# Half of the weight sums and left factors of the seven-product gemms made in earlier stages and kept in DRAM; 32 seven-product quads instead of 26

## The chip, the core and the metric

The kernel runs on one core of a Trainium2 chip. Its time is the device time of one execution in microseconds (us). Five engines run their own in-order instruction queues: TensorE (PE, matmuls; PEld is its weight load), VectorE (DVE), ScalarE (ACT), GpSimd (POOL) and SyncE (SP), which here issues nearly all DMA transfers. Semaphores tie the queues together.

## What is computed

One layer of a hybrid block for 256 tokens of width 2048: a norm, one wide projection `w_in`, an attention branch with three dilated windows, a state-space (SSM) branch with a chunked scan, a gated merge of both, and an output projection. Cut to what matters here:

```python
hn = rms_norm(x, norm_w)
proj = hn @ w_in                      # q, k, v, z_a, z_s, xbc, dt, g_a, g_s
o_a = attention(q, k, v) * silu(z_a)
y = rms_norm((scan(conv(xbc), dt) + d_skip * xs) * silu(z_s), ssm_norm_w)
merged = sigmoid(g_a) * (o_a @ w_attn_branch) + sigmoid(g_s) * (y @ w_ssm_branch)
x = x + merged @ w_out
return rms_norm(x, final_norm_w)
```

Everything is float32. The largest part of the work is the product of the 256 tokens with 2048 or 4096 rows of weights, for all the outputs.

## The kernel before

**Split products.** Each float32 operand is split into a high part (`h`, ScalarE, a copy rounded to the PE's fp32r type) and a low part (`l`, VectorE, the rest), and a product is three matmuls: high by high, high by low, low by high (`triple` in `gemm_pair`; in `gemm_a` the first two are one matmul of 512 columns, the third one of 256).

**Weights.** The host lays all weights out as 481 units of 128 x 1024 floats (512 KB) in the order of their use (`weight_plan`, `lay_weights`). `load` (L207) fetches a unit into one of four places (tag `w`) by a DMA on SP's queue; `unit` (L213) splits it into one of four places each for `h` and `l` (lines 222 and 223). The splits are put up to 120 instructions ahead of their place in the program (`L_AHEAD`). A place of `w` comes free when its `l` is made, places of `h` and `l` when their matmuls are done.

**Stages,** in the order of the PE: the first projections; the gates `gs`; the SSM part (`project` of `B`, `C`, and of 31 tiles each of `xs` and `zs`, in eight groups; beside it convolutions, decays and the scan of each group run on ScalarE and VectorE, set off by a count of ticks, `after`); then the pair stages `ssm` (columns 0 and 1024 on, `y` times `w_ssm_branch`), `v`, and half of `ga`; the attention part (`q`, `k`, `za` of 16 heads); the rest of `ga`; `attn`; `out`. The order of each engine's instructions is fixed when the program is made: a list scheduler goes by the order of the code, moved by priorities, and by its own estimate of times.

**Pair gemms and quads.** In the pair stages `gemm_pair` (L363) works in steps `q` of two row blocks of 128 (two units, 1 MB), for 2 halves of the tokens and 2 blocks of 512 columns. A plain step makes the 2x2x2 block products as 8 triples, 24 matmuls of 512 columns. A step listed in `S_QUADS` is a quad: a Winograd form with 7 triples, 21 matmuls. It needs sums of the weight blocks B11, B12, B21, B22 (line 432: B12-B11 and B12-B22 as one instruction of 1024 columns; 437: B22 minus the first; 438: B21 minus that) and four left factors, sums of the token blocks (`turn_x`, lines 355 to 360), each split into high and low again. In a quad the weight sums take places `t13` (one), `ht` and `lt` (two each) in the pool `mul`. There are 26 quads: 5 and 6 in the two halves of `ssm`, 2 and 3 in `v`, 3 in `ga`, 3 in `attn`, 2 and 2 in `out`. The left factors of `ssm` and `v` are made once per `q`, at the head of the stage that first uses them.

**Places in SBUF.** `yo0` holds the first half of `y` (`yT0`) and later `oaT`, the attention's output; `yo1` holds the raw input and norm work (`early`), later the second half of `y` (`yT1`, from group 4 on), later `v` and the `ga` gate (`vth`).

Of the kernel before, what the change touches and what calls it, by code (L numbers as in the profile page):

```python
# [31 lines left out]
MUL_PAD = 112  # L32
# [11 lines left out]
}  # L44

# [61 lines left out]
def lay_weights(mats):  # L107
    out = np.empty((N_UNITS, P, UNIT), np.float32)
    for tag, form, src, off, n_kt, w in PLAN:
# [6 lines left out]
        if form == "p":  # L116
# [3 lines left out]
            for q in range(n // 2):  # L120
                f = FIRST[tag] + 2 * q
                if q in S_QUADS[tag]:
                    out[f] = np.concatenate([m[q, 0, :, 0], m[q, 1, :, 1]], axis=1)
                    out[f + 1] = np.concatenate([m[q, 0, :, 1], m[q, 1, :, 0]], axis=1)
                else:
                    out[f : f + 2] = m[q].reshape(2, P, UNIT)
# [46 lines left out]
def hybrid_block(ctx: ExitStack, tc: tile.TileContext, wall, xt, x, pk_d, cst_d, fw_d, out):  # L173
# [15 lines left out]
    lead.tile([P, 8], F32, name="fill", tag="fill")  # L189
# [15 lines left out]
    on_unit = {}  # L205

# [6 lines left out]
    def unit(n, shape):  # L213
# [10 lines left out]
        if n in on_unit:  # L224
            on_unit.pop(n)(h[:, 0:1].bitcast(F32))
# [3 lines left out]
    def split(src, hi, lo, scale=1.0):  # L229
# [3 lines left out]
        else:  # L233
            ve.scalar_tensor_tensor(lo, src, scale, hi.bitcast(F32), ALU.mult, ALU.subtract)

# [35 lines left out]
    def gemm_dt(src):  # L271
# [8 lines left out]
        for u, tag in enumerate("hl"):  # L280
# [4 lines left out]
            if n in on_unit:  # L285
                on_unit.pop(n)(hl[:, 0, 0, 0:1].bitcast(F32))
            ve.tensor_tensor(hl[:, :, 1], w[:, ks], hl[:, :, 0].bitcast(F32), ALU.subtract)
            for kk in range(half_kt):
                kt = u * half_kt + kk
                pe.matmul(  # L290
                    acc, hl[:, kk].rearrange("p n m -> p (n m)"), src[:, kt, :], start=(kt == 0), stop=(kt == KT - 1)
# [6 lines left out]
    def gemm_first(tag, prepare, load_on):  # L298
        name = f"{tag[0]}{tag[1]}"
        accs = [bank("g", 4, f"ps_{name}_{j}") for j in range(4)]  # L300
        for u in range(KT // UB):
# [6 lines left out]
            for kk in range(UB):  # L308
                kt = u * UB + kk
                m = yT[0][:, kt, :]  # L310
# [37 lines left out]
    def turn_x(pool, bufs, temp, x, spare=0):  # L348


        sx = pool.tile([P, 2, 4 - spare, P], F32R, name=f"sx{now[0]}", tag="sx", bufs=bufs)
# [9 lines left out]
        parts = [(sx[:, 0, n], sx[:, 1, n]) for n in range(4 - spare)]  # L361
        if spare:
            own = x[:, 0, P:S], x[:, 0, S + P :]  # L363
            split(s[:, 0], *own)
            parts.insert(0, own)
        split(s[:, spare:], sx[:, 0], sx[:, 1])
        return parts

    def gemm_pair(tag, x_of, n_kt, sxs, swap, extra={}, close=1):
# [20 lines left out]
        for q in range(n_q):  # L390
            tick()
            if q in extra:
                extra[q]()
# [20 lines left out]
            for m in (n, n + 1):  # L414
                if m not in loaded:
                    load(m)
            wa, wb = loaded.pop(n), loaded.pop(n + 1)
# [11 lines left out]
            with tc.high_priority(L_AHEAD):  # L429
                t13 = mul.tile([P, UNIT], F32, name=f"t13_{n}", tag="t13", bufs=1)  # L430
                b12 = wb[:, :512].unsqueeze(1).to_broadcast([P, 2, 512])
                ve.tensor_tensor(two(t13), b12, two(wa), ALU.subtract)
# [600 lines left out]
```

## Time and profile before

| what | value |
|---|---|
| median of 3 runs | 1394.38 us (1394.28 to 1395.56) |
| span of the profiled execution | 1392.9 us (1.5 us under the median) |
| ScalarE busy | 811.5 us (58%) |
| GpSimd busy | 32.1 us (2%) |
| DMA moved | 272.33 MB, mean 196 GB/s |
| HBM read, written | 268.86 MB, 2.16 MB |

The span runs from the first to the last instruction of one execution; the runs' times hold 1.5 us around it. Busy shares are means over stages with different limits. A window's row gives, for a stretch of the span, the busy time of PE, PEld, DVE, ACT and POOL with their instruction counts, then the clock granted to the PE (1.00 is full), the DMA engines' busy share and GB/s. A row of a group gives line, engine, operation, what is written and read, shapes and count, then busy us and mean ns of one, then idle time of the engine before it and what ended it. A row of waits gives who waited for whom, us in total, times and the longest.

### The profile page before, as it was taken

The page shows a single profiled execution, that of the slowest core. Times are in us where ns is not written, and L with a number is a line of the kernel's source. Part 1 is how long each engine was busy: PE and PEld are TensorE (multiplying, and loading weights), DVE is VectorE, ACT ScalarE, POOL GpSimd, SP SyncE. Part 2 cuts the span into 40 slices and gives each one's busy share as a digit, 9 for nine tenths or more (in the row PEclk, how much of TensorE's full clock was granted, in tenths as well). Part 3 has the DMA queues.
Part 4 walks back from the last instruction along what each step waited for, and adds up shares of the span by engine and source line. Part 5 has one row for each costly group of instructions (what it writes and reads, how often), then busy time and mean ns, then how long its engine had stood idle before and what let it go on. Part 6 is the DMA issues. An engine that isn't in the chain of part 4 may idle for free.

```text
span 1392.9 us, 19889 instructions
## 1 busy us (share of the span) xinstructions
PE 1381.8 (99%) x7308; PEld 1176.8 (84%) x7308; DVE 1086.8 (78%) x1622; ACT 811.5 (58%) x1258; POOL 32.1 (2%) x86
## 2 busy tenths in 40 slices
PE   9999999999999999999999999999999999999997
PEld 7888888888888888888888888888888888888885
DVE  6897887776787787798988988766676666487887
ACT  7656676675667586665554555554554544454454
POOL 1300000000000000000000000000000000000010
PEclk9999999999999999999999999999999999999999
DMA  8766675756566665656666566655555655667564
GB/s 328 243 196 185 197 215 163 221 185 204 172 212 174 208 189 180 194 181 211 192 206 202 187 212 191 217 174 174 168 174 174 181 170 176 199 212 250 172 198 136
DMA packets 78210, 272.33 MB, mean 196 GB/s; under 512 B 8800, under 2 KB 9376, under 8 KB 77728
## 3 DMA queue, kind: packets, MB, share of 16 engines
q1 hardware_dynamic: 77392, 269.88, 61.9%
q8 instruction: 57, 0.93, 0.3%
q10 hardware_dynamic: 720, 1.18, 0.2%
q14 instruction: 41, 0.34, 0.1%
HBM read 268.86 MB, written 2.16 MB: 195 GB/s over the span
## 4 chain that ended last, share of the span: by engine, by line
PE 98%; DVE 1%; DMA 0%; issue 0%; ACT 0%; SPq 0%; POOL 0%; POOLq 0%; DVEq 0%
PE ps_zs L265 8%; PE ps_xs L265 8%; PE ps_zs L268 4%; PE ps_za L265 4%; PE ps_k L265 4%; PE ps_q L265 4%; PE ps_xs L268 4%; PE ps_ssm L384 3%; PE ps_ssm L385 3%; PE ps_ssm L386 3%; PE ps_q L268 2%; PE ps_k L268 2%; PE ps_za L268 2%; PE ps_gs L345 2%; PE ps_gs L343 2%; PE ps_gs L344 2%
## 5 line engine op out<-in xcount | busy, mean ns | idle before, releaser
L223 DVE TENSOR_TENSOR l<-w,h 128x1024 fp32r<-128x1024 f32 (+1 forms) x432 | 522.8, 1213 | 231.0 <-ACT h L222 229.3
L222 ACT ACTIVATE h<-w 128x1024 fp32r<-128x1024 f32 (+1 forms) x432 | 452.8, 1051 | 407.6 <-issue 104.5
L265 PE MATMUL ps_zs<-XT,h 128*128 128x512 f32 x496 | 174.6, 394 | 0.0
L265 PE MATMUL ps_xs<-XT,h 128*128 128x512 f32 x496 | 174.0, 393 | 0.0
L268 PE MATMUL ps_zs<-XT,l 128*128 128x256 f32 x496 | 139.2, 281 | 0.0
L268 PE MATMUL ps_xs<-XT,l 128*128 128x256 f32 x496 | 138.9, 280 | 0.0
L265 PEld LDWEIGHTS ps_zs<-XT,h 128*128 128x128 f32 x496 | 93.0, 187 | 21.3
L265 PEld LDWEIGHTS ps_xs<-XT,h 128*128 128x128 f32 x496 | 92.9, 187 | 20.9
L268 PEld LDWEIGHTS ps_zs<-XT,l 128*128 128x128 f32 x496 | 93.5, 188 | 1.2 <-issue 1.2
L268 PEld LDWEIGHTS ps_xs<-XT,l 128*128 128x128 f32 x496 | 93.5, 189 | 0.0
L265 PE MATMUL ps_q<-XT,h 128*128 128x512 f32 x256 | 92.3, 404 | 0.0
L265 PE MATMUL ps_k<-XT,h 128*128 128x512 f32 x256 | 89.8, 395 | 0.0
L265 PE MATMUL ps_za<-XT,h 128*128 128x512 f32 x256 | 89.7, 394 | 0.0
L268 PE MATMUL ps_q<-XT,l 128*128 128x256 f32 x256 | 71.1, 278 | 0.0
L268 PE MATMUL ps_za<-XT,l 128*128 128x256 f32 x256 | 71.0, 278 | 0.0
L268 PE MATMUL ps_k<-XT,l 128*128 128x256 f32 x256 | 71.0, 277 | 0.0
L385 PE MATMUL ps_ssm<-l,yT 128*128 128x512 f32 x168 | 65.3, 390 | 0.0
L386 PE MATMUL ps_ssm<-h,yT 128*128 128x512 f32 x168 | 65.0, 389 | 0.0
L384 PE MATMUL ps_ssm<-h,yT 128*128 128x512 f32 x168 | 57.5, 390 | 0.0
L265 PEld LDWEIGHTS ps_za<-XT,h 128*128 128x128 f32 x256 | 48.0, 188 | 11.3
L265 PEld LDWEIGHTS ps_k<-XT,h 128*128 128x128 f32 x256 | 48.0, 188 | 11.2
L265 PEld LDWEIGHTS ps_q<-XT,h 128*128 128x128 f32 x256 | 48.1, 188 | 10.9
(520 smaller groups left out, 2984.3 us busy)
## 6 DMA issues: line engine op xcount, KB each, us to landing
w<-in_wall SPq DMA_DIRECT2D x480, 512.0 KB, 3.8
acb<-acum_d SPq DMA_DIRECT2D x32, 256.0 KB, 3.6
th_s<-in_x SPq DMA_DIRECT2D x4, 512.0 KB, 6.5
vth<-in_x SPq DMA_DIRECT2D x1, 2048.0 KB, 9.3
early<-in_xt SPq DMA_DIRECT2D x7, 256.0 KB, 6.9
fw<-in_fw SPq DMA_DIRECT2D x1, 1024.0 KB, 5.5
out<-vth SPq DMA_DIRECT2D x4, 256.0 KB, 2.8
out<-vth ACTq DMA_DIRECT2D x4, 256.0 KB, 3.2
```

Source lines behind the costliest of these rows:

```text
L222: ac.activation(h[:, a:b], w[:, a:b], AF.Copy)
L223: ve.tensor_tensor(l[:, a:b], w[:, a:b], h[:, a:b].bitcast(F32), ALU.subtract)
L265: pe.matmul(acc, h[:, kk, :], m, start=(kt == 0), stop=False)
L268: pe.matmul(acc[:, S:], l[:, kk, :], m[:, :S], start=False, stop=(kt == KT - 1))
L343: pe.matmul(accs[i], xh, h[:, kk], start=(kt == 0), stop=False)
L344: pe.matmul(accs[i], xh, l[:, kk], start=False, stop=False)
L345: pe.matmul(accs[i], xl, h[:, kk], start=False, stop=(kt == KT - 1))
L384: pe.matmul(acc, xh, h, start=start, stop=False)
L385: pe.matmul(acc, xh, l, start=False, stop=False)
L386: pe.matmul(acc, xl, h, start=False, stop=stop)
```

## The change

The quads' lists grow to 32: 7 and 7 in `ssm`, 3 and 4 in `v`, 4 in `ga`; `attn` and `out` are unchanged. For every quad the host now lays [B11 | B21] and [B12 | B22] in its two units. Two of the sums, T1 = B12-B11 and T2 = B22-T1, are made ahead of time by `sum_weights`: it loads [B12 | B22] and B11 (768 KB), subtracts twice (128x512 each), and writes [T1 | T2] (512 KB) to DRAM. 25 such jobs run in the SSM part, one every 5 weight units from the fourth `xs` tile on, for `ssm`, `v` and `ga`; 7 run in the attention part, one every 9 units. Their places are in unused halves of the places of `y` and `o`: `yo0` and `yo1` are cut into halves `a` and `b`, and `yo1b` holds the SSM jobs' places before the last quarter of `y` needs it, `yo0b` those of attention. The left factors of `x` (4 steps, every 11 units) and of `y` (7 steps, some ticks after the group's scan) are made in the SSM part too (`keep_left`), written to DRAM and fetched back in the pair stages (`fetch_left`). In a quad, three loads (B11 with B21, [T1 | T2], B22) take the place of two, and one subtraction of 1024 columns that of three subtractions. [T1 | T2] has one place, `wt`. Three filler tiles go.

```diff
-    ("ssm", 0): (5, 7, 9, 11, 13), ("ssm", 2): (3, 5, 7, 9, 11, 13),
-    ("v", 0): (4, 6), ("v", 2): (2, 4, 6), ("ga", 2): (2, 4, 6),
+    ("ssm", 0): (4, 5, 7, 8, 10, 11, 13), ("ssm", 2): (4, 5, 7, 8, 10, 11, 13),
+    ("v", 0): (2, 4, 6), ("v", 2): (2, 4, 5, 6), ("ga", 2): (2, 4, 5, 6),
...
+SX_Y = S_QUADS[("ssm", 0)]
+SX_X = S_QUADS[("v", 2)]
+SSM_EVERY, LEFT_EVERY, ATT_EVERY = 5, 11, 9
...
+    def spill(kept, key, name, src, shape):
+        kept[key] = dram.tile([P, *shape], F32, name=name, tag=name)
+        nc.sync.dma_start(kept[key], src)
+
+    def sum_weights(tag, q, t, b11, behind):
+        n = FIRST[tag] + 2 * q
+        for dst, src in ((t, wall[n + 1]), (b11, wall[n, :, :512])):
+            gp.tensor_copy(dst[:, 0:1], behind)
+            nc.sync.dma_start(dst, src)
+        ve.tensor_tensor(t[:, :512], t[:, :512], b11, ALU.subtract)
+        ve.tensor_tensor(t[:, 512:], t[:, 512:], t[:, :512], ALU.subtract)
+        spill(presum, (tag, q), f"t_{tag[0]}{tag[1]}_{q}", t, [UNIT])
+
+    def sum_jobs(jobs, begin, every, t):
+        for n, (tag, q) in enumerate(jobs):
+            parts = t[:, n % 2], t[:, 2, n % 2 * 512 : n % 2 * 512 + 512]
+            behind_unit(begin + n * every, lambda behind, a=(tag, q, *parts): sum_weights(*a, behind))
...
+    def keep_left(key, x, spare, t):
+        sx = t.bitcast(F32R).rearrange("p (e n s) -> p e n s", e=2, n=4)[:, :, spare:]
+        turn_x(sx, t.rearrange("p (n m) -> p n m", n=2), x, spare)
+        spill(lefts, key, f"sxd_{key[0]}{key[1]}", sx.bitcast(F32), [2, 4 - spare, P])
+    def fetch_left(pool, bufs, key, x, spare):
+        sx = new_sx(pool, bufs, spare, f"{key[0]}{key[1]}")
+        nc.sync.dma_start(sx.bitcast(F32), lefts[key])
+        return left_parts(sx, x, spare)
...
-            wa, wb = loaded.pop(n), loaded.pop(n + 1)
+            wa, wc = ring(f"w{n}"), ring(f"wc{n}")
+            wt = mul.tile([P, UNIT], F32, name=f"wt{n}", tag="wt", bufs=1)
+            nc.sync.dma_start(wa, wall[n])
+            nc.sync.dma_start(wt, presum[tag, q])
+            nc.sync.dma_start(wc[:, :512], wall[n + 1, :, 512:])
...
-                t13 = mul.tile([P, UNIT], F32, name=f"t13_{n}", tag="t13", bufs=1)
-                b12 = wb[:, :512].unsqueeze(1).to_broadcast([P, 2, 512])
-                ve.tensor_tensor(two(t13), b12, two(wa), ALU.subtract)
                 ha, la = hl(stream, "a", "hl", H_BUFS)
                 part(wa, ha, la)
                 hc, lc = hl(stream, "c", "hl", H_BUFS)
-                part(wb[:, 512:], hc[:, :512], lc[:, :512])
-                ve.tensor_tensor(wb[:, :512], wa[:, 512:], t13[:, :512], ALU.subtract)
-                ve.tensor_tensor(wb[:, 512:], wb[:, 512:], wb[:, :512], ALU.subtract)
+                part(wc[:, :512], hc[:, :512], lc[:, :512])
+                t2 = wt[:, 512:].unsqueeze(1).to_broadcast([P, 2, 512])
+                ve.tensor_tensor(two(wa), two(wa), t2, ALU.subtract)
                 ht, lt = hl(mul, "t", ("ht", "lt"), 2)
-                part(t13, ht, lt)
+                part(wt, ht, lt)
                 hu, lu = hl(mul, "u", ("ht", "lt"), 2)
-                part(wb, hu, lu)
+                part(wa, hu, lu)
...
+        at = big.tile([P, 4, UNIT], F32, name="sums_ssm", tag="yo1b")
+        begin = FIRST[("xs", 4)]
+        sum_jobs(SUMS_SSM, begin, SSM_EVERY, at)
+        def left_x(q, behind):
+            gp.tensor_copy(at[:, 3, 0:1], behind)
+            keep_left(("x", q), two_kts(XT, q), 0, at[:, 3])
+        for n, q in enumerate(SX_X):
+            behind_unit(begin + 3 + n * LEFT_EVERY, lambda behind, q=q: left_x(q, behind))
...
+                    for q in (2 * g, 2 * g + 1):
+                        if q in SX_Y:
+                            after(
+                                y_lag + 2 + q % 2 * 3,
+                                lambda q=q, g=g: keep_left(
+                                    ("y", q), two_kts(yT, q), 1, at[:, 3] if g < 6 else ring(f"sxt_y{q}")
+                                ),
+                            )
...
+        sum_jobs(SUMS_ATT, FIRST[("q", 0)] + 3, ATT_EVERY, at)
```

More of the change, by code (lines that the diff above doesn't have):

```diff
@@ L360, in turn_x @@
         ve.tensor_tensor(s[:, 3], a12, s[:, 2], ALU.subtract)
[L361 removed]
         if spare:
[L363 to L365 removed]
+            split(s[:, 0], x[:, 0, P:S], x[:, 0, S + P :])
         split(s[:, spare:], sx[:, 0], sx[:, 1])
[L367 removed]
+        return left_parts(sx, x, spare)
     def gemm_pair(tag, x_of, n_kt, sxs, swap, extra={}, close=1):
@@ L836, in hybrid_block @@
     sx_of_x = {}
-    with tc.tile_pool(name="xt", bufs=1) as xtemp:
+    if True:
+        for q in SX_X:
+            sx_of_x[q] = fetch_left(xp, len(SX_X), ("x", q), two_kts(XT, q), 0)
         for c in (0, 2):
-            for q in S_QUADS[("v", c)]:
-                if q not in sx_of_x:
-                    temp = xtemp.tile([P, 2, 512], F32, name=f"sxt_x{q}", tag="tmp", bufs=1)
-                    sx_of_x[q] = turn_x(xp, 3, temp, two_kts(XT, q))
             es, prods = gemm_pair(("v", c), lambda kt: XT[:, kt, :], KT, sx_of_x, c == 2)
```

132 lines of the change are left out of this document (73 added, 59 removed).

## The prediction

> **What bounds the kernel now.** I read the page's busy shares and its chain first, then who the PE waited for, then two rows of the chain in order of time.
>
> ```profile
> span 1392.9 us, 19889 instructions
> ...
> PE 1381.8 (99%) x7308; PEld 1176.8 (84%) x7308; DVE 1086.8 (78%) x1622; ACT 811.5 (58%) x1258; POOL 32.1 (2%) x86
> ...
> PE 98%; DVE 1%; DMA 0%; issue 0%; ACT 0%; SPq 0%; POOL 0%; POOLq 0%; DVEq 0%
> ```
>
> ```profile
> PE warm L499 <- DVE ssq L496: 1.4, 1, 1.4
> PE ps_first L313 <- ACT h L222: 0.3, 1, 0.3
> ```
>
> ```profile
> 29.34 3.64 PE ps_dt L290 x16
> 606.40 0.91 PE ps_ssm L384 x4
> ```
>
> The PE is busy for 1381.8 of 1392.9 us, carries 98% of the chain, and has only two waits, 1.7 us together and both at the start. A matmul taken out of any later stage therefore shortens the span by its whole pace, as long as the operands still come in time. That pace is 3.64/16 = 0.91/4 = 0.2275 us for 512 columns.
>
> The condition is the open point, because VectorE is close behind. These windows are the start, then the SSM part from the first weight-sum jobs on (its first 108 us, and the sum over its 360.8 us in six pieces), then `ssm`, the two halves of `v`, `ga`, and attention.
>
> ```profile
> 0.00:35.00 35.00, 33.09 (x162) 27.97 (x163) 23.12 (x39) 26.66 (x49) 6.35 (x14) 1.00 0.89 329
> 140.00:248.00 108.00, 108.00 (x659) 93.73 (x658) 88.24 (x136) 76.14 (x147) 1.02 (x10) 1.00 0.64 195
> ...
> sum 360.80, PE 360.80 PEld 311.96 DVE 286.87 ACT 243.76 POOL 3.48; mean PE 60.13 PEld 51.99 DVE 47.81 ACT 40.63 POOL 0.58
> ...
> 580.00:748.00 168.00, 168.00 (x752) 139.07 (x749) 151.23 (x195) 94.48 (x109) 0.99 (x1) 1.00 0.63 199
> 748.00:790.00 42.00, 42.00 (x187) 34.80 (x186) 37.84 (x52) 22.55 (x26) 0.00 (x0) 1.00 0.59 196
> 790.00:832.00 42.00, 42.00 (x187) 34.76 (x187) 36.22 (x40) 22.41 (x25) 0.00 (x0) 1.00 0.64 201
> 832.00:873.00 41.00, 41.00 (x181) 33.71 (x180) 34.13 (x36) 21.69 (x24) 0.00 (x0) 1.00 0.60 187
> 873.00:1165.00 292.00, 292.00 (x1706) 256.59 (x1704) 193.06 (x372) 145.99 (x225) 0.00 (x0) 1.00 0.59 177
> ```
>
> VectorE is at 286.87/360.8 = 80% in the SSM part and at 259.4/293 = 89% in the pair stages, with the PE full beside it. What its idle time consists of in the SSM part, and what SP and ScalarE wait for over the whole span:
>
> ```profile
> DVE l L223 <- ACT h L222: 68.3, 60, 2.6
> ...
> SPq L211 <- DVE l L223: 486.1, 227, 8.6
> ...
> ACT h L222 <- DMA w<-in_wall: 24.5, 22, 3.7
> ```
>
> Of the 73.9 idle us, 68.3 are waits for the next `h`, and those mostly for a place that the PE frees: VectorE is ahead, not starved. Loads are seldom late: 22 of 432 splits waited for one.
>
> **The change, part by part.**
>
> **Matmuls.** 32 quads for 26, each with 21 matmuls for 24: 6 x 3 = 18 fewer, 18 x 0.2275 = **4.10 us**, all on the path: 2 + 1 quads in `ssm`, 1 + 1 in `v`, 1 in `ga`. [...] The order of the products in a quad costs nothing: they are the same 21 matmuls.
>
> **VectorE in the pair stages.** The durations:
>
> ```profile
> L223 DVE TENSOR_TENSOR l<-w,h 128x1024 fp32r<-128x1024 f32 x73 | 89.1, 1223 | 16.9 <-ACT h L222 16.4
> L432 DVE TENSOR_TENSOR t<-w,w 128x1024 f32<-128x1024 f32 x19 | 23.3, 1225 | 14.4 <-DMA w<-in_wall 14.3
> ...
> L426 DVE TENSOR_TENSOR ltt<-t,htt 128x1024 fp32r<-128x1024 f32 x19 | 23.2, 1221 | 0.0
> ...
> L438 DVE TENSOR_TENSOR w<-w 128x512 f32<-128x512 f32 x19 | 13.0, 687 | 0.0
> L437 DVE TENSOR_TENSOR w<-w,t 128x512 f32<-128x512 f32 x19 | 13.0, 686 | 0.0
> L426 DVE TENSOR_TENSOR lc<-w,hc 128x512 fp32r<-128x512 f32 x19 | 13.0, 686 | 0.3 <-ACT hc L425 0.3
> ...
> L355 DVE TENSOR_TENSOR sxt_y<-yT 128x512 f32<-128x512 f32 x6 | 4.1, 688 | 0.0
> L232 DVE TENSOR_TENSOR sx<-sxt_y,sx 128x384 fp32r<-128x384 f32 x6 | 3.3, 555 | 0.0
> L232 DVE TENSOR_TENSOR sx<-sxt_x,sx 128x512 fp32r<-128x512 f32 x3 | 2.1, 689 | 0.1
> L355 DVE TENSOR_TENSOR sxt_x<-XT 128x512 f32<-128x512 f32 x3 | 2.1, 687 | 0.0
> ...
> L357 DVE TENSOR_TENSOR sxt_y<-sxt_y 128x128 f32<-128x128 f32 x6 | 1.7, 290 | 0.0
> ```
>
> A quad costs VectorE now 1.225 + 3 x 1.221 + 3 x 0.686 = 6.95 us, more than its 21 x 0.2275 = 4.78 us of PE. Afterwards it is 1.225 + 3 x 1.221 + 0.686 = 5.57. A left factor of `y` is 0.688 + 5 x 0.290 + 0.555 = 2.69, one of `x` 0.687 + 4 x 0.290 + 0.689 = 2.54. The stages from 580 to 873 us change by 6 x (5.57 - 2 x 1.223) = +18.7, 19 x (-1.38) = -26.2 and -(6 x 2.69 + 3 x 2.54) = -23.8: 259.4 becomes 228.1 of 288.9 us, 79%. This saves nothing by itself, since the PE is already full.
>
> **VectorE in the SSM part.** Added: 25 jobs of two 512-wide subtractions, 25 x 1.373 = 34.3; four left factors of `x`, 10.2; six of `y` inside the 360.8 us, 16.1 (the seventh comes later). Together 60.6 us into 73.9 idle, 96% busy. It is tightest at the head: the jobs come every 5 units, at about 3 us a unit, and all four of `x` lie there, so 140 to 248 us takes 7.2 x 1.373 + 10.2 = 20.1 us into 19.8 idle. Packed instructions overlap by 0.08 us each (first two rows below: 143.63 + 1.22 against 144.77), which gives some 3.5 us back: 104.8 of 108 us. The work is hidden, if VectorE's idle time can really be used. What the PE has as cover, at the leanest unit of the three groups I followed (49: its `l` ends at 144.85, its first low matmul starts at 147.44), and at a quad of `ga`:
>
> ```profile
> 143.63 1.22 DVE L223 TENSOR_TENSOR l<-w,h 128x1024 fp32r<-128x1024 f32 x1
> 144.77 0.42 DVE L328 SCALAR_TENSOR_TENSOR xs<-th_x,cv_x 128x256 f32<-128x256 f32 x1
> ```
>
> ```profile
> 147.44 0.36 PE L268 MATMUL ps_xs<-XT,l 128*128 128x256 f32 x1
> ```
>
> ```profile
> 853.46 1.22 DVE L426 TENSOR_TENSOR ltt<-t,htt 128x1024 fp32r<-128x1024 f32 x1
> ```
>
> ```profile
> 855.55 0.39 PE L385 MATMUL pp_ga<-ltt,sx 128*128 128x512 f32 x1
> ```
>
> The cover is 2.6 us in the SSM part and 0.87 us at that quad. If VectorE's time were not free, the SSM work would cost up to its 60.6 us; I take 0, since what is added goes into waits for `h` that end by themselves, and the splits keep their priority.
>
> **ScalarE, GpSimd, attention.** ScalarE gets two copies per left factor, under 1.5 us each, beside 117 idle us. GpSimd, busy for 3.48 us, gets one-column copies; the clearing of `raw`, which the convolutions need, stands behind them, but their places were left two jobs earlier. Seven jobs in attention are 9.6 us of VectorE in 98.9 idle. All taken at 0.
>
> **DMA and queues.**
>
> ```profile
> w<-in_wall SPq DMA_DIRECT2D x480, 512.0 KB, 3.8
> ...
> out<-vth ACTq DMA_DIRECT2D x4, 256.0 KB, 3.2
> ```
>
> A job moves 768 KB in and 512 KB out, 1.31 MB; 25 of them and ten left factors (4.5 MB) put 37 MB into 360.8 us, 103 GB/s on the present 195. The first 35 us carried 329 GB/s, so 298 passes, with later landings. A write of 512 KB to DRAM isn't in the trace; the nearest row is 3.2 us for 256 KB, and a job's place is wanted again only after 10 units, 30 us. On SP's queue a job adds two loads and a write that waits for the second subtraction, with the next weight loads behind it. A quad has three loads for two, 1.31 MB in 4.78 us.
>
> The load of [T1 | T2] has a price. `wt` has one place, so in neighbouring quads the next load waits until `ltt` of this one is made, and `wc` and later loads stand behind it on SP. One round is 3.8 (landing) + 1.22 (subtraction) + 1.22 (`ltt`) = 6.3 us against 4.78 of PE: 1.5 us of cover lost per neighbour. `ssm` has three couples in each half, with a plain step after each to recover; `v` and `ga` have one run of three (4, 5, 6), two losses in a row, 3.0 us. With cover of 3 us the cost is 0, with the 0.87 of the row 2.2 us a run. The 0.87 belongs to a VectorE at 83% (34.13/41) with dearer quads; I take 0.25 a run, **0.5 us** in all, ends 0 and 4.3.
>
> **Sum.** Against the profiled execution 1392.9 - 4.1 + 0.5 = 1389.3 us of span; the median lies 1.5 us above its span, so **1390.8 us**.
>
> **The rivals.**
>
> *One place for wt.* The runs of three lose 2.2 us each: 1394.4 - 4.1 + 4.3 = 1394.6, no change. For it: the 0.87 us, and the 14.3 us that line 432 waited for loads. Against it: the first quad of a run finds its sums loaded long before, and VectorE has more air.
>
> *VectorE becomes the bound in the SSM part* (slower). The 60.6 us, less 0.08 us for each of some 120 instructions, are 51 packed. If only a share s of the 73.9 idle us is usable, since each `l` must follow its `h` and a subtraction that waits for its load holds up every split behind it, the PE loses 51 - 73.9 s less 2.6 of cover. With s = 0.5 that is 11.5 us: 1394.4 - 4.1 + 11.5 = 1401.8. It decides from s = 0.56 down, where the loss passes 6.9 us; above 0.64 it is under 1.3. For it: 97% at the head. Against: the long row of waits for `h`, and windows at 89% without a PE wait.
>
> *SP's queue.* A write of sums stands on SP until VectorE has subtracted; loads behind it go out late. If half of the 25 jobs cost the PE 1 us beyond its cover, 12 us: 1402. Against it: SP itself waits 486 us for places, so it has time, and loads have been early.
>
> *It saves no PE time.* Not possible here as I read it: the 18 matmuls are gone, and nothing is added to the PE.
>
> **How the numbers follow.** A measurement of this kernel tells some 0.2%, 2.8 us, from no change: faster is under 1391.6, slower over 1397.2. Forecast (up to 1.3 us given back): 0.53. One place for `wt`: 0.20, all of it no change. VectorE in the SSM part: 0.20, of which 0.02 falls within 0.2%. SP's queue: 0.07, slower. So faster 0.53, same 0.22, slower 0.25. The likeliest case alone runs from 1390.0 to 1391.6. The range for 8 in 10 starts at 1389.8 (no cost, and 0.5 us of spread as the runs show) and takes in the `wt` case and the milder part of the VectorE case, up to 1399.
>
> **What would show it.** The matmul lines of `pp` and `ps` should have 18 fewer instructions. Right: the PE still has no wait after the start, and VectorE stands near 96% from 140 to 500 us and near 79% in the pair stages. Wrong by `wt`: PE gaps at steps 5 and 6 of `v` and `ga` that end with `ltt` or `ltu`. Wrong by VectorE: gaps in `xs` and `zs` ended by `l`. Wrong by SP: `h` waiting for the load of `w` in the SSM part.

## The result and the profile after

The changed kernel takes 1417.3 us (median of 4 runs, 1411.6 to 1422.2) against 1395.0 for the kernel before beside it: a ratio of 1.0158, 95% interval 1.0131 to 1.0185. It is 1.6% slower; the prediction said 1390.8 us with a range up to 1399. The profiled execution has a span of 1414.2 us.

First the page of the changed kernel, its span, the PE's row and the chain that ended last:

```profile
span 1414.2 us, 20374 instructions
...
PE 1390.0 (98%) x7290; PEld 1176.2 (83%) x7290; DVE 1109.6 (78%) x1665; ACT 818.9 (58%) x1273; POOL 66.2 (5%) x154
...
PE 68%; DMA 15%; DVE 7%; ACT 5%; issue 3%; SPq 0%; POOL 0%; DVEq 0%; POOLq 0%; ACTq 0%
DMA sums_ssm<-in_wall 5%; DMA w<-in_wall 5%; PE ps_k L304 4%; PE ps_za L304 4%; PE ps_q L304 4%; DMA acb<-acum_d 4%; PE ps_zs L304 3%; PE ps_xs L304 3%; PE ps_ssm L437 3%; PE ps_ssm L438 3%; PE ps_ssm L439 3%; DVE l L252 2%; PE ps_q L307 2%; PE ps_k L307 2%; PE ps_za L307 2%
```

The PE has 7290 instructions, 18 fewer, as forecast. But it carries 68% of the chain, no longer 98%, and three kinds of loads carry 14%: those of the sum jobs, of the weights, and of `acb` (the decays). GpSimd's busy time has doubled, from 32.1 to 66.2 us.

Where the time went is read from the first PE instruction of each stage in the trace. The last column is a trial explained below (`e17`): the changed kernel without the one-column copies of the SSM part's sum jobs, and with 30 quads instead of 32:

| stretch, us | before | after | without the copies |
|---|---|---|---|
| up to the first `xs` matmul | 76.8 | 77.3 | 77.4 |
| SSM part | 503.9 | 525.7 | 508.9 |
| `ssm` | 167.7 | 165.6 | 165.6 |
| `v` to the end | 644.6 | 645.6 | 643.1 |
| span | 1392.9 | 1414.2 | 1394.9 |

The SSM part lost 21.8 us, the stages from `v` on became 1.0 us longer where they should have become shorter, and only `ssm` came out as planned: 3 quads x 3 x 0.2275 = 2.05 us, measured 2.1. The same stretch of the SSM part in the windows view of before and of after, and of the trial (columns: length, busy us of PE, PEld, DVE, ACT, POOL, clock, DMA share, GB/s):

```profile
115.00:520.00 405.00, 405.00 (x2415) 351.02 (x2414) 320.68 (x484) 278.50 (x521) 3.88 (x38) 1.00 0.63 193
```

```profile
115.00:520.00 405.00, 393.91 (x2291) 335.33 (x2290) 342.99 (x558) 264.03 (x498) 31.48 (x90) 1.00 0.82 273
```

```profile
115.00:520.00 405.00, 405.00 (x2393) 349.33 (x2393) 357.14 (x576) 279.12 (x529) 6.92 (x39) 1.00 0.82 274
```

After the change the PE stands still for 11 us here, while VectorE has 62 us of idle time and DMA runs at 273 GB/s. In the third row, VectorE does more in the same 405 us and DMA moves just as much, and the PE is full. So neither of the two is at a limit in the changed kernel.

The 11 us of waits are half of the 21.8 us. The other half is a slower pace: over the whole SSM part, with the same 2982 matmuls, the windows view has the PE busy for 503.90 us before, 514.61 us after and 508.80 us in the trial. The 5 us that the trial keeps are taken up under "The remainder", and up to 1.7 us are a lower clock (last section); the other 4 us were not traced.

The waits of the same stretch, before and after (who waited for whom: us in total, times, longest):

```profile
DVE l L223 <- ACT h L222: 77.0, 64, 4.0
...
ACT gt L650 <- DMA acb<-acum_d: 16.8, 14, 2.8
...
ACT h L222 <- DMA w<-in_wall: 3.1, 3, 1.4
```

```profile
POOL sums_ssm L225 <- ACT h L251: 80.9, 19, 16.2
DVE sums_ssm L227 <- DMA sums_ssm<-in_wall: 42.2, 22, 4.3
...
ACT h L251 <- DMA w<-in_wall: 35.2, 25, 5.1
...
ACT gt L706 <- DMA acb<-acum_d: 29.2, 17, 3.5
...
DVE l L252 <- ACT h L251: 15.5, 16, 2.7
```

```profile
SPq L226 <- POOL sums_ssm L225: 33.9, 23, 4.4
...
SPq L219 <- DVE sums_ssm L228: 28.0, 18, 3.7
```

VectorE's 77 us of waits for `h` were to take up the new work. 15.5 us of them are left, but 42 us are now waits for the loads of the jobs, 22 of 25 times. ScalarE waits 35 us for weights that came in time before. SP's queue stands 34 us behind the one-column copies (line 225) and 28 us behind the second subtraction (line 228). No engine waits for the clearing of `raw`, which stands behind the copies on GpSimd.

One job in the timeline, the same stretch of GpSimd, SP and VectorE (start, us, engine, line, what; idle time before and its end in brackets):

```profile
223.79 1.36 POOL L225 COPY sums_ssm<-h 128x1 f32<-128x1 f32 x2 [1.52 <-ACT h L251]
```

```profile
225.06 0.80 SPq L226 DMA_DIRECT2D sums_ssm<-in_wall  x2
225.97 8.30 SPq L240 DMA_DIRECT2D w<-in_wall  x3
234.88 0.33 SPq L219 DMA_DIRECT2D t_ssm<-sums_ssm  x1
```

```profile
231.69 0.69 DVE L227 TENSOR_TENSOR sums_ssm<-sums_ssm 128x512 f32<-128x512 f32 x1 [2.52 <-DMA sums_ssm<-in_wall]
```

The copies wait for `h` of the job's own unit. Only then, at 225.06, does SP issue the two loads, and at 225.97 the weights behind them. The job's loads land 6.15 us later (the chain's row, below), when VectorE has stood at the subtraction for 2.52 us with the splits of the next units behind it. This chain shows what follows, in order of time (start, us, what):

```profile
224.49 0.95 ACT h L251
225.44 6.15 DMA sums_ssm<-in_wall
...
235.26 4.51 DMA acb<-acum_d
241.68 5.96 DMA acb<-acum_d
...
257.99 5.99 DMA w<-in_wall
```

One late load is followed by the next: `w` and `acb` stand in the same queue. In SP's rows above, `w` goes out 0.11 us after the job's loads (225.06 + 0.80, then 225.97), and `acb` 0.05 us after the write (234.88 + 0.33, then 235.26).

### The profile page after: what moved, and what is told of

The parts are those of the page before. It is cut to its first block, busy times and chain, and to the rows that moved or that the text cites. A ratio compares the mean times of both kernels' runs of the same rounds, so it can differ in the third digit from the quotient of the medians.

```text
span 1414.2 us, 20374 instructions
## 1 busy us (share of the span) xinstructions
PE 1390.0 (98%) x7290; PEld 1176.2 (83%) x7290; DVE 1109.6 (78%) x1665; ACT 818.9 (58%) x1273; POOL 66.2 (5%) x154
## 4 chain that ended last, share of the span: by engine, by line
PE 68%; DMA 15%; DVE 7%; ACT 5%; issue 3%; SPq 0%; POOL 0%; DVEq 0%; POOLq 0%; ACTq 0%
DMA sums_ssm<-in_wall 5%; DMA w<-in_wall 5%; PE ps_k L304 4%; PE ps_za L304 4%; PE ps_q L304 4%; DMA acb<-acum_d 4%; PE ps_zs L304 3%; PE ps_xs L304 3%; PE ps_ssm L437 3%; PE ps_ssm L438 3%; PE ps_ssm L439 3%; DVE l L252 2%; PE ps_q L307 2%; PE ps_k L307 2%; PE ps_za L307 2%
## 5 line engine op out<-in xcount | busy, mean ns | idle before, releaser
L251 ACT ACTIVATE h<-w 128x1024 fp32r<-128x1024 f32 (+1 forms) x420 | 438.5, 1048 | 360.8 <-DMA w<-in_wall 69.6
L252 DVE TENSOR_TENSOR l<-w,h 128x1024 fp32r<-128x1024 f32 (+1 forms) x420 | 507.0, 1211 | 150.4 <-ACT h L251 148.8
L304 PE MATMUL ps_zs<-XT,h 128*128 128x512 f32 x496 | 177.5, 398 | 0.6 <-ACT h L251 0.6
L706 ACT ACTIVATE gt<-acb,acT 128x128 f32<-128x128 f32 x128 | 44.3, 391 | 33.9 <-DMA acb<-acum_d 30.9
L480 DVE TENSOR_TENSOR la<-w,ha 128x1024 fp32r<-128x1024 f32 x32 | 39.0, 1220 | 18.1 <-ACT ha L479 17.7
L479 ACT ACTIVATE htt<-wt 128x1024 fp32r<-128x1024 f32 x32 | 33.8, 1055 | 29.0 <-DMA wt<-t_ssm 9.2
```

The costliest lines, as they stand in the source:

```text
L251: ac.activation(h[:, a:b], w[:, a:b], AF.Copy)
L252: ve.tensor_tensor(l[:, a:b], w[:, a:b], h[:, a:b].bitcast(F32), ALU.subtract)
L304: pe.matmul(acc, h[:, kk, :], m, start=(kt == 0), stop=False)
L479: ac.activation(h, src, AF.Copy)
L480: ve.tensor_tensor(l, src, h.bitcast(F32), ALU.subtract)
L706: ac.activation(g4[:, n, b], acb[:, j, b // 2 * P : b // 2 * P + P], AF.Relu, scale=-1.0, bias=sc[:, h : h + 1],)
```

## The experiments

Each kernel was run beside the kernel before (1394.6 to 1395.4 us). "SSM part" is the length in its profiled execution, 503.9 us before, 525.7 after.

### First series: which work of the jobs is it?

Three kernels leave out the traffic (`e1`), the subtractions (`e2`), or both (`e6`); the copies stay. With thin loads the places are cleared once by GpSimd beforehand, and the quads load plain weights in place of the sums.

```diff
 e1, e6:
-            nc.sync.dma_start(dst, src)
+            nc.sync.dma_start(dst[:, :64], src[:, :64])
-        spill(presum, (tag, q), f"t_{tag[0]}{tag[1]}_{q}", t, [UNIT])
+        spill(presum, (tag, q), f"t_{tag[0]}{tag[1]}_{q}", t[:, :64], [64])
 e2, e6:
-        ve.tensor_tensor(t[:, :512], t[:, :512], b11, ALU.subtract)
-        ve.tensor_tensor(t[:, 512:], t[:, 512:], t[:, :512], ALU.subtract)
```

> Leaves out most of the data of the sum jobs: each load and each write moves 64 of the 512 or 1024 columns, and the quads load other weights in place of the sums; all VectorE, ScalarE and GpSimd instructions stay. Theory A (the subtractions stop VectorE's queue until their loads land, and the jobs' 1.31 MB each make the other loads late): the PE gaps of the SSM part go, about 18 of the 24 us lost come back, 1398 us or less. Theory B (VectorE's own time in the SSM part is too much, about 97% full): the gaps stay, 1412 to 1418 us.

> Leaves out the two subtractions of all 32 sum jobs; loads, writes and left factors stay, and the write waits for the loads alone. Theory A1 (VectorE's queue stops at the subtraction): the SSM gaps go, about 1398 us. Theory A2 (the DMA traffic makes the loads of w and acb late, whatever VectorE does): most of the gaps stay, over 1408 us. Theory B (VectorE's time): half of the added time is gone, 1398 to 1404 us.

> Leaves out both: the data of the sum jobs (64 columns move) and their subtractions; only the left factors are still made in the SSM part. If the two causes add (thin loads gave back 9 us, no subtractions 9 us of the 22), the SSM part loses 4 us or less and the time is 1396 to 1400 us. If a third cause matters (the left factors, the order of the instructions), it stays over 1404 us.

Measured: `e1` 1408.3 us, 1.0094 (1.0079 to 1.0109), SSM part 516.5; `e2` 1408.7 us, 1.0096 (1.0077 to 1.0115), 515.0; `e6` 1399.5 us, 1.0040 (1.0025 to 1.0055), 509.7. The waits of `e1` and of `e2` from 115 to 520 us:

```profile
DVE sums_ssm L227 <- DMA sums_ssm<-in_wall: 42.1, 20, 3.7
```

```profile
ACT h L249 <- DMA w<-in_wall: 46.5, 27, 3.9
...
ACT gt L704 <- DMA acb<-acum_d: 34.4, 15, 5.5
```

And SP's wait for the copies in `e6`:

```profile
SPq L226 <- POOL sums_ssm L225: 51.4, 25, 4.1
```

Without the traffic VectorE stops just as long, 42.1 us: the loads are late however small they are. Without the subtractions VectorE doesn't stop, but weights and decays are late. Each gives back some 10 us and both together 16. I read this as two causes that add up. That fell later: both are needs of the same kind, and what makes both late had stayed in all three kernels. `e6` also shows that SP's stop behind the copies is not a price by itself: with thin loads and no subtraction SP stands 51.4 us behind them, and only 5.8 us are lost.

### Second series: moving one thing at a time

`e3` and `e12` tie the subtraction to a unit three later, by a zero made on GpSimd or on ScalarE; `e4` makes no left factors (a clearing of their place by GpSimd stands there); `e5` issues the loads of `acb` from ScalarE's queue; `e7` subtracts on GpSimd; `e11` issues the jobs' loads from GpSimd's queue and has quads 2, 4, 6 in the second half of `v` and in `ga`.

```diff
 e12 (e3 alike, with two operations of gp for the zero):
+        zero = lead.tile([P, 1], F32, name=f"zero{tag[0]}{tag[1]}_{q}", tag="zero", bufs=2)
+        ac.activation(zero, behind, AF.Copy, scale=0.0)
-        ve.tensor_tensor(t[:, :512], t[:, :512], b11, ALU.subtract)
+        ve.scalar_tensor_tensor(t[:, :512], t[:, :512], zero, b11, ALU.add, ALU.subtract)
+            behind_unit(begin + n * every + 3, lambda behind, a=(tag, q, *parts): sum_weights(*a, behind))
 e4:
-        turn_x(sx, t.rearrange("p (n m) -> p n m", n=2), x, spare)
+        gp.memset(t, 0.0)
 e5:
-            nc.sync.dma_start(acb, acum_d[2 * t : 2 * t + 2, :].partition_broadcast(P))
+            nc.scalar.dma_start(acb, acum_d[2 * t : 2 * t + 2, :].partition_broadcast(P))
 e7:
-        ve.tensor_tensor(t[:, :512], t[:, :512], b11, ALU.subtract)
+        gp.tensor_tensor(t[:, :512], t[:, :512], b11, ALU.subtract)
 e11:
-            nc.sync.dma_start(dst, src)
+            gp.dma_start(dst, src)
```

> The same work as the changed kernel, but the subtractions of a job are tied to the weight unit three after its loads, so that VectorE reaches them when the loads have landed. Theory A1: VectorE no longer waits for the sum loads (42 us before), the SSM gaps go, 1395 to 1400 us. Theory A2 or B: unchanged, 1412 to 1418 us.

> Leaves out the making of the eleven left factors in the SSM part (27 us of VectorE); a place of zeros is written to DRAM and fetched instead. Theory A1: the waits at the sum loads remain, the loss shrinks little, 1408 to 1416 us. Theory B: 27 of the 61 us are gone and the head of the part has room, 1398 to 1402 us.

> The changed kernel with the loads of the decays' sums (acb) issued from ScalarE's queue in place of SP's; nothing is left out. Theory A2 (in the SSM part the loads are late, and acb, which has one place and stands on SP behind the jobs' loads and writes, holds ScalarE and with it the splits): the gaps shrink, 1403 to 1411 us. Theory A1 alone (only VectorE's stop at the subtraction counts): 1413 to 1420 us.

> The same work, with the two subtractions of each job on GpSimd in place of VectorE, so that GpSimd's queue and not VectorE's stops for the sum loads. A1 and A2 both: like the kernel without subtractions, 1404 to 1412 us. If GpSimd's stop matters in its turn (the clearing of raw stands behind it), 1412 us or more.

> The changed kernel with the jobs' loads issued from GpSimd's queue, and with v's and ga's second halves at quads 2, 4, 6 (no run of three; two quads fewer). Theory: VectorE's stop and the traffic stay, so the SSM part loses nearly as much as before (18 to 23 us); v and ga lose nothing against the kernel before, which gives back about 3 us there, less 0.46 for two quads: 1413 to 1416 us. Rival (SP's queue, in which the jobs' writes wait for the subtraction and the kernel's own loads stand behind): the SSM part's loss falls by 5 us or more, 1405 to 1409.

> The subtraction of each job is tied to a unit three later, by way of a tiny zero made on ScalarE at that unit (GpSimd has no part in it), so the loads have landed when VectorE comes to it. Theory (VectorE stopping for the loads is about half of the loss): VectorE's idle time before the subtraction goes from 42 us to under 10, and the time is near that of the kernel without subtractions, 1405 to 1410 us. Rival (the subtractions' own time or the traffic decides): 1413 to 1418 us.

Measured, with the SSM part's length: `e3` 1415.3 us, 1.0147 (1.0132 to 1.0162), 524.3; `e4` 1420.3 us, 1.0178 (1.0161 to 1.0195), 531.7; `e5` 1415.2 us, 1.0144 (1.0111 to 1.0177), 522.7; `e7` 1417.0 us, 1.0157 (1.0142 to 1.0173), 525.1; `e11` 1415.5 us, 1.0138 (1.0118 to 1.0158), 528.9; `e12` 1413.7 us, 1.0134 (1.0120 to 1.0148), 520.8.

None gives back more than 5 us of the SSM part. `e12` is the telling miss. VectorE no longer waits for the job's loads at all, as meant, and still 16.9 us of the 21.8 are lost, with these waits from 115 to 520 us:

```profile
DVE l L256 <- ACT h L255: 49.3, 30, 4.4
ACT h L255 <- DMA w<-in_wall: 46.0, 23, 4.9
```

```profile
SPq L225 <- POOL sums_ssm L224: 51.7, 27, 5.0
```

The wait has moved from VectorE to ScalarE; SP still stands behind the copies. `e11` settles two things. From `v` to the end it takes 643.2 us against 645.6, with two quads fewer: without runs of three quads nothing is lost there. And with the loads off SP's queue the SSM part doesn't gain: 25.0 us are lost. The copies still hold the loads (GpSimd waits 144.3 us for `h` at them), VectorE still stops for 44.9 us, and SP now waits 36.5 us with the writes behind the subtraction. `e3` and `e4` put more on GpSimd and are no clean tests. `e5` is unclear within its interval, `e7` the same as the changed kernel (its rows are in the last section).

### Third series: how many jobs, and the left factors alone

`e8`, `e9` and `e10` make T1 and T2 inside the quad from the units that are loaded anyway, all left factors in the SSM part as in the change: `e8` for all 32 quads, `e9` for 28 that are two apart, `e10` for 24 of 30, with six jobs left, one every 20 units.

```diff
+            for m in (n, n + 1):
+                if m not in loaded:
+                    load(m)
+            wa, wt = loaded.pop(n), loaded.pop(n + 1)
+                part(wt[:, 512:], hc[:, :512], lc[:, :512])
+                ve.tensor_tensor(wt[:, :512], wt[:, :512], wa[:, :512], ALU.subtract)
+                ve.tensor_tensor(wt[:, 512:], wt[:, 512:], wt[:, :512], ALU.subtract)
-        sum_jobs(SUMS_SSM, begin, SSM_EVERY, at)
```

> The 32 quads and the moved left factors stay, but no weight sums are made ahead: each quad loads its two units and makes T1 and T2 in place (VectorE 6.95 us a quad as before, 2 loads, no place wt). Both theories of the SSM part: its loss goes, 3 us or less is left from the left factors. The pair stages get about 91% of VectorE; if neighbours pass, 1392 to 1397 us; if they stall there, 1398 to 1405 us.

> 28 quads of seven products, always two apart (SSM part 3, 5, 7, 9, 11, 13 in both halves, v 2, 4, 6 in both, ga 2, 4, 6 in the second), left factors made in the SSM part as in the changed kernel, and the sums of the weights made on VectorE inside each quad from the tiles that are there anyway; no job loads or writes anything. Theory (the sum jobs, their loads that VectorE stops for and their traffic, are the whole loss; the left factors cost nothing): the SSM part starts its pair stage within 1 us of the kernel before (580.7), no stage loses over 0.5 us, and 14 more quads save 14 x 0.2275 = 3.2 us less than the kernel before has of its own, so about 1393 us against 1395. Rival (VectorE is too full for the left factors beside the loads): the SSM part still loses some us and the whole is at or above 1395.

> 30 quads, but only six jobs (quads 5, 8 and 11 of the SSM part's pair stages), one every 20 units; the sums of the other quads are made in place. Theory that the loss is proportional to the jobs: 6/25 of 22 us = 5 us in the SSM part, 2.7 us saved by matmuls, about 1397. Theory that a loss comes only where jobs come close together (the DMA engines over 0.85 busy): the SSM part loses at most 1 us and the whole is about 1392 to 1394, if quads 4-5, 7-8 and 10-11 hold without a stall; those stalls would show in the pair stages' own start times.

The expectation of `e9` counts wrongly: 28 quads are two more than before, not 14, and save 1.4 us.

Measured: `e8` 1417.0 us, 1.0160 (1.0144 to 1.0175), SSM part 506.4, `ssm` 180.8; `e9` 1401.3 us, 1.0043 (1.0030 to 1.0055), SSM part 504.0, `ssm` 168.0, `v` to the end 649.1; `e10` 1404.0 us, 1.0065 (1.0052 to 1.0077), SSM part 507.0, `ssm` 169.2, `v` to the end 648.4.

`e8` and `e10` are slower than either theory of their expectations allowed. In the SSM part the nine left factors of `e9` cost nothing, 504.0 against 503.9 us. But `e8`, with eleven left factors and no job, loses 2.5 us there without a PE wait, and `e10`, with ten left factors and six jobs, 3.1 us. So what a job costs can't be read from `e10`, and not all of the loss comes from the jobs; the larger part of the 21.8 us does. And the jobs serve a purpose: with the sums made in place, neighbouring quads stall (`e8` takes 13.1 us longer in `ssm` than before, with 3 quads more). `e9` is not faster either, for `v` to the end takes 4.5 us more than before; why was not followed up.

### Fourth series: the copies

What the kernels that lose most have in common are the copies on GpSimd that hold a job's loads until unit n is split. `e13` to `e15` drop them and let the loads stand in SP's own order at unit n, the subtractions at n + 3, the write at n + 8 (30 quads: `v` and `ga` with 2, 4, 6); `e14` thins the loads and writes as `e1`, `e15` leaves the subtractions out. The edit sets the order of the program; by the trace the scheduler undid both lags: in `e13` the write goes out right behind the second subtraction (0.0 us after it in the median), as in the changed kernel.

```diff
-            gp.tensor_copy(dst[:, 0:1], behind)
...
+            for f, lag in ((sum_load, 0), (sum_weights, 3), (sum_keep, 8)):
+                behind_unit(begin + n * every + lag, lambda behind, f=f, a=(tag, q, *parts): f(*a))
```

> The jobs without the one-column copies on GpSimd: the two loads stand on SP's queue in the order of the program at unit n, the subtractions on VectorE at unit n + 3, the write on SP at unit n + 8, so that SP stops neither for a split nor for a subtraction; v's and ga's second halves at quads 2, 4, 6 (30 quads, 2.7 us of matmuls less than the kernel before). Theory (SP's queue, held 34 us by the copies and 39 us by the writes, is the 5 to 6 us that were left without traffic and without subtractions): VectorE waits under 10 us for the sum loads, SP's waits for the copies are gone, and the SSM part loses about 10 us more than the kernel before instead of 22: 1401 to 1404 us. Rival (the remainder lies elsewhere): the SSM part loses 16 us or more, as with the subtractions tied late: 1408 to 1413.

> The same, but the jobs move 64 columns of each tile (the quads then load other weights in place of the sums). No stop, no traffic, a free queue; only the subtractions' own 34 us on VectorE and the left factors are left. Theory: the SSM part loses at most 4 us more than the kernel before: 1392 to 1396 us. Rival (VectorE's own time is a price by itself): the loss stays at 6 us or more: 1399 or above.

> The same with full loads and writes, but without the subtractions (the quads then take plain weights in place of T1 and T2). Only the traffic is left. Theory: DMA at 270 GB/s or more, splits wait 30 us or more for w, and the SSM part loses 5 to 8 us more than the kernel before: 1397 to 1400 us. Rival (traffic does harm only by way of a held queue): under 2 us are lost, 1392 to 1395.

Measured: `e13` 1400.4 us, 1.0033 (1.0021 to 1.0044), SSM part 508.9; `e14` 1413.8 us, 1.0126 (1.0109 to 1.0142), 524.3; `e15` 1403.9 us, 1.0060 (1.0045 to 1.0075), 510.6.

`e13` gives back 16.8 us of the SSM part with every byte and every subtraction in place: the same 274 GB/s from 115 to 520 us, and VectorE at 357.24 us. The price of traffic and of VectorE's time that `e1` and `e2` seemed to show was a price of their lateness. `e15`, with less work, is no faster than `e13`; it missed its range, and ScalarE waits 3.9 us there for weights where 30 were expected. `e14` missed: it moves less and is slow again. SP's timeline in it shows another order, so that it tells nothing on traffic:

```profile
177.86 3.29 SPq L224 DMA_DIRECT2D sums_ssm<-in_wall  x3
181.20 0.42 SPq L243 DMA_DIRECT2D w<-in_wall  x1
...
185.60 1.25 SPq L243 DMA_DIRECT2D w<-in_wall  x1
...
191.47 0.90 SPq L243 DMA_DIRECT2D w<-in_wall  x2
```

With small transfers the order on SP came out different, jobs bunched ahead of weights: two weight units go out in the 13.6 us from 177.86 to 191.47, where the kernel before issues one every 3.0 us (135 from 115 to 520 us). ScalarE then waits 3.8 us for a weight, up to 197.23, and the PE 5.4 us, up to 202.00; the rest of its 20.4 us was not traced. An edit that thins a load also changes the order that the list scheduler makes, and `e1` and `e6` may have part of their time from that.

`e13` loses 3.6 us in `ssm` (169.2 against 165.6), where the chain has `wt`:

```profile
714.75 8.09 DMA wt<-t_ssm
```

The attention jobs, no longer paced, were loaded there too. The last three kernels put that right and take the parts of `e13` one by one, all with 30 quads and attention's jobs paced as in the change (in `e18` by its copies, too): `e16` is `e13` otherwise; `e17` only drops the copies of the SSM part; `e18` keeps them and puts subtraction and write at n + 3 and n + 8.

```diff
 e17:
-            gp.tensor_copy(dst[:, 0:1], behind)
+            if paced:
+                gp.tensor_copy(dst[:, 0:1], behind)
 e18:
             gp.tensor_copy(dst[:, 0:1], behind)
             nc.sync.dma_start(dst, src)
...
+            for f, lag in ((sum_load, 0), (sum_weights, 3), (sum_keep, 8)):
+                behind_unit(begin + n * every + lag, lambda behind, f=f, a=(tag, q, *parts): f(*a, behind))
```

> Jobs of the SSM part in SP's own order as in the last trial (loads at unit n, subtractions at n + 3, write at n + 8), those of attention paced by the copies as in the changed kernel; 30 quads. In the last trial the attention jobs, unpaced, were loaded in the last third of the ssm stage and the sums of quads 10, 11 and 13 landed 5 to 8 us after their issue. Theory: that was the 3.6 us lost in the ssm stage, which goes to under 0.5; the SSM part loses 4 to 6 us as there: 1396 to 1398 us. Rival (the ssm stage loses because sums and left factors are written later): the 3.6 us stay, 1400.

> Of the three things that the in-order trial changed at once only one: the one-column copies of the SSM part's weight jobs are gone, so the loads aren't held back to the split of unit n; subtractions and write follow the loads directly, as in the changed kernel; 30 quads. Theory (the copies delay the loads until VectorE already stands at the subtraction, and hold SP): VectorE's waits for the sum loads fall from 42 us to under 10, and the SSM part's loss from 22 us to 5 to 8, 1397 to 1401 us. Rival (the writes, which wait on SP for the subtraction, are at least half): 1404 to 1409.

> The other part: copies stay, subtractions at unit n + 3 and write at n + 8; 30 quads. Theory (the copies are the larger part): SP still waits 30 us or more for the copies, and the SSM part loses 12 us or more: 1404 to 1410. Rival (the writes and the stop at the subtraction are the larger part): the SSM part loses 5 to 8 us: 1397 to 1401.

Measured: `e16` 1396.5 us, 1.0012 (1.0003 to 1.0021), SSM part 508.9, `ssm` 165.6; `e17` 1396.8 us, 1.0014 (1.0005 to 1.0023), 508.9, 165.6; `e18` 1415.2 us, 1.0145 (1.0131 to 1.0159), 526.2, 165.7. The waits of `e17`, then of `e18`, from 115 to 520 us:

```profile
ACT gt L707 <- DMA acb<-acum_d: 10.2, 10, 2.1
ACT h L252 <- DMA w<-in_wall: 5.9, 6, 3.0
...
DVE sums_ssm L228 <- DMA sums_ssm<-in_wall: 2.7, 4, 1.1
```

```profile
DVE sums_ssm L228 <- DMA sums_ssm<-in_wall: 45.8, 20, 4.3
```

```profile
SPq L225 <- POOL sums_ssm L224: 41.9, 26, 4.2
```

`e17` and `e18` are the pair that settles it, both with 30 quads and 23 jobs: without the 46 copies of one column the SSM part loses 5.0 us, with them 22.3. Against the changed kernel, `e17` brings back 16.8 of the 21.8 us. `e18` is no test of the write, though. The scheduler undid its lags as in `e13`: by the trace's start times the subtraction begins 5.9 us after the issue of the second load (median; 6.2 in the changed kernel), and the write goes out right behind the second subtraction. What speaks against the write as a cause of its own is `e17`: it stands behind the subtraction there too, SP waits for it only 12.3 us (28.0 in the changed kernel), and `e16`, whose lags were undone too, has the same length.

All three kinds of late loads go with the copies, though in `e17` the jobs' loads take no less time than in the changed kernel, which its page's DMA issues show beside those of the changed kernel (KB each, median us to landing):

```profile
sums_ssm<-in_wall SPq DMA_DIRECT2D x23, 512.0 KB, 6.5
```

```profile
sums_ssm<-in_wall SPq DMA_DIRECT2D x25, 512.0 KB, 5.6
```

They are issued earlier: the subtraction begins 9.7 us after the issue of the second load (median), so the load has landed. Nothing paces them any more, either: the last job's write goes out at 331 us, in the changed kernel at 505. Whether it also helps that the jobs leave the last part free was not tried by itself; from 248 to 331 us, with jobs, the PE has no wait. `e17`'s attention jobs keep their copies and `ssm` loses nothing.

The gain of 30 quads is 12 x 0.2275 = 2.7 us, and the SSM part still takes 5.0 us more than before. So `e16` and `e17` stay 1.9 and 2.2 us behind the kernel before, and no version run here beats it.

## Why the prediction was wrong

**Matmuls: right.** 18 fewer instructions (x7290), and `ssm` is shorter by 2.1 us for 2.05 forecast.

**VectorE in the pair stages: right.** Forecast 228.1 of 288.9 us, 79%. The sum of the four windows from 603 to 890 us after the change:

```profile
sum 287.00, PE 285.82 PEld 235.08 DVE 228.67 ACT 159.28 POOL 0.70; mean PE 71.45 PEld 58.77 DVE 57.17 ACT 39.82 POOL 0.17
```

**The work in the SSM part: the capacity right, the price of 0 not.** "The work is hidden, if VectorE's idle time can really be used": `e17` shows that it can be used without a PE wait, but 5.0 us are lost all the same (below). Its windows view for the tightest 108 us, where 104.8 us of VectorE were forecast:

```profile
140.00:248.00 108.00, 108.00 (x644) 92.62 (x644) 101.59 (x166) 75.71 (x143) 4.09 (x12) 1.00 0.95 335
```

VectorE is 94% busy and DMA moves 335 GB/s, above the forecast 298, with the PE at 108.00 of 108; 11 jobs fall into this stretch where 7 were forecast. "298 passes, with later landings" holds too. The forecast of 96% of VectorE from 140 to 500 us does not: it was 306.56 of 360 us, 85%, after the change, and 88% in `e17`. Over the whole part its busy time rose by 48.4 us, near the 51 that the second rival gave for packed instructions and not the 60.6 of the forecast.

**The step that failed** stands under ScalarE, GpSimd, attention: "GpSimd, busy for 3.48 us, gets one-column copies; the clearing of `raw`, which the convolutions need, stands behind them ... All taken at 0." I asked what is queued behind a copy on GpSimd, not what waits for it: the job's load, and with it all of SP's queue behind that load. The copy waits for `h` of the job's own unit, so it takes from the loads the lead that hid their 6 us: 6.2 us from issue to use with the copies, 9.7 without. Not 0 but 16.8 us came back when the copies went. How much of it goes by VectorE's stop and how much by SP's stays open: in `e11` SP didn't stand behind the copies and the loss stayed, in `e6` it did and the loss was small. The rival on SP's queue named the neighbouring wait, the write behind the subtraction, at a chance of 0.07 and 12 us; `e17` shows that this wait shrinks by itself when the loads are early, and in no run did the write alone move. The sentence in the second rival, "a subtraction that waits for its load holds up every split behind it", describes what VectorE then did (42.2 us), but it was priced as a share of idle time that can't be used, and with early loads that share is high.

**`wt`: the mechanism right in part, the size off.** I took 0.5 us for the two runs of three, with ends at 0 and 4.3. From `v` to the end the kernel should have become 9 x 0.2275 = 2.05 us shorter and became 1.0 longer: 3.0 us lost. The PE's waits from 845 to 893 us after the change, 2.1 us in all, are in `ga` and at its end; the run of three in `v` shows none:

```profile
PE ps_ga L437 <- ACT hc L479: 1.1, 1, 1.1
...
PE ps_q L304 <- ACT h L251: 0.6, 1, 0.6
PE pp_ga L437 <- ACT htt L479: 0.4, 1, 0.4
```

They end with high parts of ScalarE, not with `ltt` or `ltu` as forecast. The chain before the first of them begins with `wt`, but its last load is that of `wc`:

```profile
863.65 4.47 DMA wt<-t_ga
...
874.58 1.24 DVE ltu L480
875.83 4.49 DMA wc<-in_wall
```

The late `wt` made its quad late, and `wc` of the second quad after it went out only when `ltu` of this quad was made, which frees a place of `w`. That second place was not in the forecast.

In `e11`, `e16` and `e17`, without runs of three, the loss is gone. The couples in `ssm` cost nothing, as said.

**The remainder, 5.0 us in the SSM part of `e17`, stays open.** The profile shows no PE wait there; the windows of that stretch above do show 2393 matmuls where before there were 2415 in 405.00 us of "busy" PE, so a full row can hide a slower pace. By the trace's start times two groups take longer from one start to the next: the 128 matmuls of 128 columns that make the scan's `yp`, 9.7 us for 7.8, and the 1984 of the projections `xs` and `zs`, 350.0 us for 347.2. The scan's matmuls also stand in another order: neighbours among them differ in width 101 times, 67 times before. `e9` has 67 and loses nothing; `e8`, which has no jobs, has 95 and loses 2.5 us. So about half of the remainder may come without any job. That the order is the cause was not tried by itself.

## What to carry to other kernels

A transfer that was "paced" here by a tiny instruction (two copies take 1.36 us in the timeline above) waited in two queues, that of the tiny instruction's engine (80.9 us for `h` on GpSimd) and that of the issuing engine (33.9 us for the copies on SP), and VectorE stood 42.2 us at the subtraction that needed it: price the wait, not the copy. Here it was enough to leave such loads in the queue's own order; look at the time from issue to use, 6.2 us with the copies and 9.7 without. A lag written into the program is not yet a lag on the chip: read from the trace whether an edit moved anything before calling it a test. When leaving out either of two parts helps, and each by half, look for what both wait for before calling them two causes.

## What the runs showed of the hardware

**GpSimd beside VectorE.** In `e7` the two subtractions of 128x512 took GpSimd 1762 and 1620 ns (VectorE: 692 and 685 in the changed kernel), and some of VectorE's own instructions grew. Two of its groups in the changed kernel, then in `e7`:

```profile
L685 DVE SCALAR_TENSOR_TENSOR cv_x<-raw_x,cw,cv_x 128x256 f32<-128x256 f32 x93 | 44.6, 479 | 1.6 <-ACT cv_x L683 0.7
...
L756 DVE TENSOR_TENSOR y<-y,zs 128x512 f32<-128x512 f32 x16 | 11.0, 689 | 0.3
```

```profile
L685 DVE SCALAR_TENSOR_TENSOR cv_x<-raw_x,cw,cv_x 128x256 f32<-128x256 f32 x93 | 51.3, 552 | 1.6 <-ACT cv_x L683 0.4
...
L756 DVE TENSOR_TENSOR y<-y,zs 128x512 f32<-128x512 f32 x16 | 14.2, 889 | 0.0
```

The means of these went from 479 to 552 ns and from 689 to 889 ns. `lc` of the quads, 128x512 in stages without such subtractions, stayed at 685. By what way GpSimd's subtractions lengthen VectorE's instructions is not shown.

**The PE's clock after a short wait.** In the changed kernel the PE waited 2.4 us for one `l` shortly before 256 us (the longest wait of line 307), and then ran at a lower granted clock (the third value from the end of the row: 1.00, then 0.57):

```profile
250.00:256.00 6.00, 3.31 (x18) 2.50 (x17) 5.74 (x11) 4.76 (x13) 0.00 (x0) 1.00 0.66 194
256.00:260.00 4.00, 4.00 (x14) 3.47 (x15) 3.00 (x4) 4.00 (x8) 0.00 (x0) 0.57 0.53 133
```

The clock records put it at 0.5 for 3.4 us, so up to 1.7 us were lost there beyond the wait itself. The wait was 2.4 us in one piece, 2.7 us within the 6 us. The PE's other waits in this execution are of 1.5 us at most; from 7 us on, the clock records give 1.00 behind each of them. That the wait lowered the clock is my reading of this one case; it was not tried by itself.
